# Nine transposes of the scan's decays, sums and steps into one PSUM tile, in one row, with two copies behind them

## The chip, the core and the metric

The kernel runs on one core of a Trainium2 chip, as one program in one launch. The metric is the device time in microseconds (us) of that launch; lower is better. The engines of the core work side by side, each through its own queue in order: TensorE (PE, with PEld for its weight loads), VectorE (DVE), ScalarE (ACT), GpSimd (POOL) and SyncE (SP, which here only issues transfers). They wait for each other by semaphores.

## What is computed

One layer of a streaming encoder for 256 prompt frames and 32 sample frames (288 columns together): a projection `w_in`, a pooling mixer, a state-space mixer, `w_out`, and a convolutional feed-forward part (`w_up`, `w_down`), each with RMS norms. The part around the change is the state-space scan. Cut to what matters:

```python
dt = softplus(dt_raw + dt_bias)                   # 32 heads x positions
a = dt * -exp(a_log); acum = cumsum(a)            # per chunk
lmat = exp(where(causal, acum_l - acum_s, -inf))
y_diag = einsum(cb, lmat, x * dt)                 # cb = C B^T
decay_states = exp(acum_last - acum)
states = einsum(B, decay_states, x * dt)
y = y_diag + C h_prev exp(acum) + D * x
```

## The kernel before

All activations lie with features on the 128 partitions and the 288 positions in the free dimension. A weight matrix is fetched in pieces (`raw`), split into a high part `whi` by ACT (L129) and a low part `wlo` by DVE (L130), and every 128x128 block takes three products of 288 columns (L135, L136, L137, the main stream): high with high, high with low, low with high. A piece is 128x1024 and serves 24 products. `project` runs this over column groups of 256; in the stretch of the change the groups are those of `xs` (the scan's input) and then those of `z` (its gate).

Between the products of the main stream PE does the scan's own small products in plain f32. `g` (sums of dt*A), `dt` (steps) and `dec` (decays times steps) are 32 heads by positions. The scan needs them with positions on the partitions, so nine transposes of 32 rows turn them (L412 to L414): three blocks of positions by the three quantities, the last block of `dec` from a copy of it, `dec_s` (L408). Two DVE copies per block bring them to SBUF: `tok` (sums and steps, L415) and `tokd` (decays, L416). PSUM tiles named `aux` come from a ring of three. Two other users: `pcb` (L429 to L431: the C B^T products, which DVE masks into `cbt`, L432 to L435) and `py` (L475 to L481: the scan's output).

`ssd_four(q)` does four heads. SP loads `gb` (the sums, broadcast) and `xw` (the input, positions on partitions, read back from the DRAM tile `xs_d`). DVE scales `xw` by the steps (L458). ACT forms `m` with the sums of `tok` as its bias (L463) and takes its exponential (L466), DVE multiplies it by `cbt` (L468), and PE forms `py`. The DRAM tile `xs_d` is written block by block: `conv_out` makes a tile of xs (DVE L346, L351, L352; ACT L344, L350), and `blocks_out` turns it in 32x32 blocks on DVE into the tile `blocks`, of which there is one buffer, and stores it with four transfers on SP's queue:

```python
170  s = pool_.tile([P, NT], F32, tag="blocks", bufs=1, name="blocks")
171  dve.transpose(s, src)
172  dv = d[:, t * P : (t + 1) * P].rearrange("(j r) (i f) -> i r j f", r=32, f=32)
173  for i in range(4):
174      sp.dma_start(out=dv[i], in_=s[32 * i : 32 * (i + 1), :].rearrange("r (j f) -> r j f", f=32))
```

What order the instructions take on each engine is not the order of the code. The kernel is recorded with `schedule_with_timeline_sim` set: a scheduler deals the recorded instructions into the engines' queues by a model of their times, as soon as what they read is there by that model. `tc.keep_in_program_order(ins)` binds an instruction to stay behind the one recorded before it on its engine. The queues are fixed when the program is built; on the chip nothing is reordered.

Of the kernel before, what the change touches and what calls it, by code (L numbers as in the profile page):

```python
# [16 lines left out]
P = 128  # L17
# [4 lines left out]
NT = NP_ + NS  # L22
# [3 lines left out]
HEADS = 32  # L26
# [17 lines left out]
def body(  # L44
# [25 lines left out]
    act, dve, pool, pe, sp = nc.scalar, nc.vector, nc.gpsimd, nc.tensor, nc.sync  # L70
# [11 lines left out]
    def aux(shape, name):  # L82
        return aux_ps.tile(shape, F32, tag="aux", name=name)
# [4 lines left out]
    def btile(name):  # L88
        return bpool.tile([P, NT], F32, tag="b", name=name)
# [202 lines left out]
    p_ = aux([P, NT], "pdt")  # L292
# [23 lines left out]
    id32 = ident[:HEADS, :HEADS]  # L316
# [45 lines left out]
    def htile(name, n=NT, tag=None):  # L362
        return mp.tile([HEADS, n], F32, tag=tag or name, name=name, bufs={"z": 4}.get(tag, 2) if tag else 1)
# [16 lines left out]
    dt = htile("dt", tag="gsum")  # L380
# [7 lines left out]
    g = mp.tile([HEADS, 2, MW], F32, tag="m", bufs=2, name="g")[:, 0, :]  # L388
# [11 lines left out]
    dec = htile("dec", tag="gsum")  # L400
# [4 lines left out]
    tok = mp.tile([P, 3, 2, HEADS], F32, name="tok")  # L405
    tokd = const.tile([P, 3, HEADS], F32, name="tokd")
    dec_s = mp.tile([HEADS, 4, NS], F32, name="dec_s")
    dve.tensor_copy(dec_s, dec[:, NP_:].unsqueeze(1).broadcast_to([HEADS, 4, NS]))  # L408
    dec_s = dec_s.rearrange("h r s -> h (r s)")
    for b, (go, o) in enumerate(((0, 0), (256, P), (288, NT - P))):  # L410
        p_ = aux([P, 3, HEADS], "ptok")
        pe.transpose(p_[:, 0, :], g[:, go : go + P], id32)  # L412
        pe.transpose(p_[:, 1, :], dt[:, o : o + P], id32)
        pe.transpose(p_[:, 2, :], dec_s if b == 2 else dec[:, o : o + P], id32)  # L414
        dve.tensor_copy(tok[:, b, :, :], p_[:, 0:2, :])  # L415
        dve.tensor_copy(tokd[:, b, :], p_[:, 2, :])  # L416

    bc = []
    for i in range(4):
        o = btile("bc")  # L420
# [5 lines left out]
    for gi in range(2):  # L426
        blocks_out(b_d, gi, bc[gi], mp)
        p_ = aux([P, MW], "pcb")
# [546 lines left out]
    for m in range(0, KD, 2):  # L975
        for p_ in project(wdv[:, :, 0:HALF, :], [(m * P, 256)], f[:HALF], [(0, 8), (8, 8), (16, 6)]):
            o = btile("part")
# [263 lines left out]
```

## Time and profile before

| | |
|---|---|
| median of 3 runs | 1320.14 us (1319.52 to 1320.19) |
| the profiled execution's own time | 1319.83 us |
| its span, first to last instruction | 1318.0 us |
| busy: PE / DVE / ACT / POOL | 1311.0 / 895.2 / 671.9 / 225.8 us |
| granted clock of PE over the span | 0.999 |
| the nine transposes stand between | 98.6 and 106.5 us |

A row of the trace in order of time reads: start, duration (both us, the start from the begin of the span), engine, line of the code, operation, what is written and read, shape, count; in square brackets the idle time of the engine before it and what ended that. Consecutive instructions of one line are merged in a row. PE's durations overlap: the next product starts before the last one has left the array. So the distance between two starts is what a product costs.

### The profile page before, as it was taken

How to read it: one execution, taken by the hardware profiler on the slowest of the kernel's cores; microseconds unless marked ns; L12 is line 12 of the kernel's file. 1: busy time of each engine (PE TensorE's matmuls, PEld its weight loads, DVE VectorE, ACT ScalarE, POOL GpSimd, SP SyncE). 2: the span in 40 equal slices, each digit the busy share in tenths (PEclk: the TensorE clock that was granted, in tenths of full speed). 3: DMA queues.
4: the chain of work that ended last, by engine and by line, in shares of the span. 5: the costliest groups of instructions: out<-in, count | busy, mean ns of one | idle time of the engine just before them, and what ended most of it. 6: DMA issues, size and time to landing. Idle time of an engine off the chain costs nothing.

```text
span 1318.0 us, 25197 instructions
## 1 busy us (share of the span) xinstructions
PE 1311.0 (99%) x10067; PEld 1298.9 (99%) x10067; DVE 895.2 (68%) x1486; ACT 671.9 (51%) x1010; POOL 225.8 (17%) x363
## 2 busy tenths in 40 slices
PE   9999999999999999999999999999999999999998
PEld 9999999999999999999999999999999999999997
DVE  7999988779654599977766743346666666664544
ACT  7558867446543466644444433334444454444443
POOL 6321211221430200211211200001111111101110
PEclk9999999999999999999999999999999999999999
DMA  8668874465665556666544445445444554466663
GB/s 320 209 210 283 265 235 147 151 227 205 204 216 186 181 169 220 186 184 194 174 163 161 157 171 174 155 175 181 172 160 164 179 171 160 164 235 186 204 179 109
DMA packets 104564, 249.81 MB, mean 190 GB/s; under 512 B 64224, under 2 KB 69792, under 8 KB 82176
## 3 DMA queue, kind: packets, MB, share of 16 engines
q1 hardware_dynamic: 102352, 243.44, 56.1%
q0 software_dynamic: 1664, 4.59, 1.2%
q8 instruction: 78, 1.28, 0.4%
q14 instruction: 38, 0.31, 0.1%
q10 hardware_dynamic: 432, 0.19, 0.1%
HBM read 236.23 MB, written 11.95 MB: 188 GB/s over the span
## 4 chain that ended last, share of the span: by engine, by line
PE 98%; DMA 1%; ACT 0%; DVE 0%; issue 0%; SPq 0%; ACTq 0%
PE acc L135 31%; PE acc L137 31%; PE acc L136 31%; DMA raw<-in_w_first 1%; PE py L475 1%; PE acc_x L135 1%; PE acc_x L137 1%; PE acc_x L136 1%; PE pst L772 0%; PE run_a L1113 0%; PE low L1111 0%; PE run_b L1126 0%; PE py L477 0%; PE pdt L296 0%; PE py L481 0%; PE py L479 0%
## 5 line engine op out<-in xcount | busy, mean ns | idle before, releaser
L130 DVE TENSOR_TENSOR wlo<-raw,whi 128x1024 fp32r<-128x1024 f32 (+1 forms) x386 | 463.3, 1201 | 316.0 <-ACT whi L129 313.6
L129 ACT ACTIVATE whi<-raw 128x1024 fp32r<-128x1024 f32 (+1 forms) x386 | 400.3, 1038 | 471.0 <-PE acc L136 373.9
L135 PE MATMUL acc<-hn,whi 128*128 128x288 f32 x1360 | 393.3, 294 | 0.0
L136 PE MATMUL acc<-hn,whi 128*128 128x288 f32 x1360 | 392.7, 293 | 0.0
L137 PE MATMUL acc<-hn,wlo 128*128 128x288 f32 x1360 | 392.0, 293 | 0.0
L135 PEld LDWEIGHTS acc<-hn,whi 128*128 128x128 f32 x1360 | 253.3, 188 | 0.4 <-ACT hn L872 0.4
L136 PEld LDWEIGHTS acc<-hn,whi 128*128 128x128 f32 x1360 | 253.4, 188 | 0.1
L137 PEld LDWEIGHTS acc<-hn,wlo 128*128 128x128 f32 x1360 | 253.3, 188 | 0.0
L135 PE MATMUL acc<-xn,whi 128*128 128x288 f32 x688 | 202.8, 297 | 0.6 <-ACT whi L275 0.6
L136 PE MATMUL acc<-xn,whi 128*128 128x288 f32 x688 | 200.6, 293 | 0.0
L137 PE MATMUL acc<-xn,wlo 128*128 128x288 f32 x688 | 196.0, 295 | 0.0
L135 PE MATMUL acc<-fa,whi 128*128 128x288 f32 x660 | 194.0, 294 | 0.0
L136 PE MATMUL acc<-fa,whi 128*128 128x288 f32 x660 | 193.4, 293 | 0.0
L137 PE MATMUL acc<-fa,wlo 128*128 128x288 f32 x660 | 193.1, 293 | 0.0
L135 PEld LDWEIGHTS acc<-xn,whi 128*128 128x128 f32 x688 | 129.5, 188 | 2.3 <-issue 0.9
L136 PEld LDWEIGHTS acc<-xn,whi 128*128 128x128 f32 x688 | 129.3, 188 | 0.4
L137 PEld LDWEIGHTS acc<-xn,wlo 128*128 128x128 f32 x688 | 126.9, 188 | 0.0
L135 PEld LDWEIGHTS acc<-fa,whi 128*128 128x128 f32 x660 | 124.1, 188 | 0.0
L137 PEld LDWEIGHTS acc<-fa,wlo 128*128 128x128 f32 x660 | 123.9, 188 | 0.0
L136 PEld LDWEIGHTS acc<-fa,whi 128*128 128x128 f32 x660 | 123.9, 188 | 0.0
L924 POOL COPY fc_stage<-ebuf 128x4 f32<-128x4 f32 x88 | 28.2, 320 | 521.4 <-DVE ebuf L923 521.4
L920 POOL COPY ebuf<-pf 128x2 f32<-128x2 f32 x88 | 72.3, 822 | 125.3 <-DVE fc L930 76.1
(307 smaller groups left out, 1737.6 us busy)
## 6 DMA issues: line engine op xcount, KB each, us to landing
raw<-in_w_up SPq DMA_DIRECT2D x80, 1024.0 KB, 4.8
raw<-in_w_in SPq DMA_DIRECT2D x38, 1024.0 KB, 5.0
raw<-in_w_down SPq DMA_DIRECT2D x32, 1024.0 KB, 4.7
raw<-in_w_out SPq DMA_DIRECT2D x23, 1024.0 KB, 4.8
raw<-in_w_down SPq DMA_DIRECT2D x16, 768.0 KB, 4.3
raw<-in_w_up SPq DMA_DIRECT2D x8, 896.0 KB, 4.5
gb<-g_d SPq DMA_DIRECT2D x8, 832.0 KB, 6.3
raw<-in_w_first SPq DMA_DIRECT2D x6, 768.0 KB, 8.0
```

The source lines that it names most:

```text
L129: act.activation(hi, raw[:, k : k + n, :], AF.Copy)
L130: dve.tensor_tensor(lo, raw[:, k : k + n, :], hi.bitcast(F32), op=ALU.subtract)
L135: pe.matmul(out, wh, a[:, 0, :], start=start, stop=False)
L136: pe.matmul(out, wh, a[:, 1, :], start=False, stop=False)
L137: pe.matmul(out, wl, a[:, 0, :], start=False, stop=stop)
L475: pe.matmul(y[:, 0:256], xw[:, 0, c], m[:, j, 0:256], start=True, stop=False)
L920: pool.tensor_copy(e[:, 258:260], pf[:, 4:6, i])
L924: pool.tensor_copy(fc_stage[:, :, :, i], e[:, 256:324].rearrange("p (s c) -> p s c", c=34)[:, :, 0:2])
```

## The change

The nine transposes write one PSUM tile of 128 x 3 x 3 x 32, in one fixed row: first the three of the decays, beginning with `dec_s`, then sums and steps block by block. Each but the first is bound to stay behind the one before. One copy brings all sums and steps to `tok`, one all decays to `tokd`.

```diff
-    for b, (go, o) in enumerate(((0, 0), (256, P), (288, NT - P))):
-        p_ = aux([P, 3, HEADS], "ptok")
-        pe.transpose(p_[:, 0, :], g[:, go : go + P], id32)
-        pe.transpose(p_[:, 1, :], dt[:, o : o + P], id32)
-        pe.transpose(p_[:, 2, :], dec_s if b == 2 else dec[:, o : o + P], id32)
-        dve.tensor_copy(tok[:, b, :, :], p_[:, 0:2, :])
-        dve.tensor_copy(tokd[:, b, :], p_[:, 2, :])
+    def tok_out():
+        p_ = aux([P, 3, 3, HEADS], "ptok")
+        jobs = [(2, 2, dec_s)] + [(b, 2, dec[:, P * b : P * b + P]) for b in range(2)]
+        for b, (go, o) in enumerate(((0, 0), (256, P), (288, NT - P))):
+            jobs += [(b, 0, g[:, go : go + P]), (b, 1, dt[:, o : o + P])]
+        for n, (b, i, src) in enumerate(jobs):
+            ins = pe.transpose(p_[:, b, i, :], src, id32)
+            if n:
+                tc.keep_in_program_order(ins)
+        dve.tensor_copy(tok, p_[:, :, 0:2, :])
+        dve.tensor_copy(tokd, p_[:, :, 2, :])
+
+    tok_out()
```

Six more lines of code shift the lines behind: L416 is then the transposes, L419 and L420 are the copies, and L429 becomes L435, L458 L464, L468 L474, L475 L481.

The scheduler deals the queues anew from this place on. On PE, in the group of `xs` where the transposes stand, six of the nine came before in two places:

```order
L137 MATMUL acc<-xn,wlo 128x288
L412 MATMUL ptok<-ident,g 128x32
L413 MATMUL ptok<-ident,dt 128x32
L135 MATMUL acc<-xn,whi 128x288
L412 MATMUL ptok<-ident,g 128x32
L413 MATMUL ptok<-ident,dt 128x32
L412 MATMUL ptok<-ident,g 128x32
L413 MATMUL ptok<-ident,dt 128x32
L136 MATMUL acc<-xn,whi 128x288
```

Two of the decays followed 33 products of the main stream later, and `dec_s` another 15 later. Now, six products of the main stream behind the place where `dec_s` stood:

```order
L135 MATMUL acc<-xn,whi 128x288
L416 MATMUL ptok<-ident,dec_s 128x32
L416 MATMUL ptok<-ident,dec 128x32 x2
L416 MATMUL ptok<-ident,g 128x32
L416 MATMUL ptok<-ident,dt 128x32
L416 MATMUL ptok<-ident,g 128x32
L416 MATMUL ptok<-ident,dt 128x32
L416 MATMUL ptok<-ident,g 128x32
L416 MATMUL ptok<-ident,dt 128x32
L435 MATMUL pcb<-bc 128x256
```

All nine stand together, and the six products of `pcb`, which stood 18 products of the main stream behind `dec_s`, follow at once.

On DVE, the stretch in which the product m of the first four heads stands (L468, now L474), before:

```order
L351 SCALAR_TENSOR_TENSOR xs<-tanh,conv 128x256
L352 SCALAR_TENSOR_TENSOR xs<-tanh,conv 128x32
L468 TENSOR_TENSOR m<-m,cbt 128x1664
L351 SCALAR_TENSOR_TENSOR xs<-tanh,conv 128x256
L171 STREAM_TRANSPOSE blocks<-xs 128x288
L352 SCALAR_TENSOR_TENSOR xs<-tanh,conv 128x32
L130 TENSOR_TENSOR wlo<-raw,whi 128x1024
L468 TENSOR_TENSOR m<-m,cbt 128x1664
L130 TENSOR_TENSOR wlo<-raw,whi 128x1024
L346 SCALAR_TENSOR_TENSOR conv<-ebuf_111,pah,conv 128x291
L130 TENSOR_TENSOR wlo<-raw,whi 128x1024
L171 STREAM_TRANSPOSE blocks<-xs 128x288
```

And now:

```order
L351 SCALAR_TENSOR_TENSOR xs<-tanh,conv 128x256
L352 SCALAR_TENSOR_TENSOR xs<-tanh,conv 128x32
L130 TENSOR_TENSOR wlo<-raw,whi 128x1024
L351 SCALAR_TENSOR_TENSOR xs<-tanh,conv 128x256
L352 SCALAR_TENSOR_TENSOR xs<-tanh,conv 128x32
L171 STREAM_TRANSPOSE blocks<-xs 128x288
L474 TENSOR_TENSOR m<-m,cbt 128x1664
L130 TENSOR_TENSOR wlo<-raw,whi 128x1024
L171 STREAM_TRANSPOSE blocks<-xs 128x288
```

The first m moved behind the turning of the second tile of its pair, and the turning after that follows closer; the second m comes further on. Further up in the same queue the two copies stand six rows later than the first pair of the old ones did: behind four steps of the convolution, the product for `ce` and one more weight piece.

The third place is `py` of heads 4 to 7 on PE. Before it stood in two halves with main stream between them, each of them:

```order
L135 MATMUL acc<-xn,whi 128x288
L475 MATMUL py<-m,xw 64x256 x2
L477 MATMUL py<-m,xw 64x128 x2
L479 MATMUL py<-m,xw 64x32 x2
L481 MATMUL py<-ce,h0t 64x32 x2
L136 MATMUL acc<-xn,whi 128x288
```

Now it is one piece:

```order
L135 MATMUL acc<-xn,whi 128x288
L481 MATMUL py<-m,xw 64x256 x4
L483 MATMUL py<-m,xw 64x128 x4
L485 MATMUL py<-m,xw 64x32 x4
L487 MATMUL py<-ce,h0t 64x32 x4
L136 MATMUL acc<-xn,whi 128x288
```

The `py` of the first four heads stands eleven products of the main stream further on than before. From the `py` of heads 8 to 11 on, PE's small products stand within one product of their old places in the main stream.

## The prediction

> **What bounds the kernel now.** I read the page first, then the busy time by window, then the order of time of PE and of DVE around the change, and last the waits of DVE.
>
> ```profile
> span 1318.0 us, 25197 instructions
> PE 1311.0 (99%) x10067; PEld 1298.9 (99%) x10067; DVE 895.2 (68%) x1486; ACT 671.9 (51%) x1010; POOL 225.8 (17%) x363
> PE 98%; DMA 1%; ACT 0%; DVE 0%; issue 0%; SPq 0%; ACTq 0%
> ...
> 125.00:155.00 30.00, 30.00 (x268) 28.76 (x265) 26.99 (x50) 26.65 (x58) 6.22 (x7) 1.00 0.85 269
> ...
> 183.00:213.00 30.00, 30.00 (x247) 29.51 (x247) 29.36 (x44) 20.32 (x40) 9.12 (x8) 1.00 0.63 192
> ```
>
> The first three lines say that PE sets the time: 99% busy, 98% of the chain that ended last. So a cut of PE's own work counts in full, and any wait that reaches PE counts in full too. The two rows by window (PE, weight load, DVE, ACT, POOL busy, then clock and DMA share) say where such a wait could come from. DVE is 68% busy as a mean, but from 183 to 213 us it works 29.36 of 30.00 us. There it has nothing left with which to make up for being late.
>
> **What the change takes off PE.** A product of the main stream with 288 columns starts every 0.131 us: in the rows below 24 steps lie between 100.72 and 103.86. What an insertion costs is the distance between a product before it and a product two places behind it, less the steps of the main stream in between.
>
> ```profile
> 98.40 0.29 PE L137 MATMUL acc<-xn,wlo 128*128 128x288 f32 x1
> ...
> 99.92 0.30 PE L135 MATMUL acc<-xn,whi 128*128 128x288 f32 x1
> ...
> 100.72 0.29 PE L135 MATMUL acc<-xn,whi 128*128 128x288 f32 x1
> ...
> 103.86 0.29 PE L135 MATMUL acc<-xn,whi 128*128 128x288 f32 x1
> 104.09 0.31 PE L414 MATMUL ptok<-ident,dec 32*128 32x32 f32 x2
> ...
> 104.69 0.30 PE L135 MATMUL acc<-xn,whi 128*128 128x288 f32 x1
> ...
> 106.28 0.29 PE L135 MATMUL acc<-xn,whi 128*128 128x288 f32 x1
> 106.51 0.24 PE L414 MATMUL ptok<-ident,dec_s 32*128 32x32 f32 x1
> ...
> 107.05 0.29 PE L135 MATMUL acc<-xn,whi 128*128 128x288 f32 x1
> ```
>
> One transpose alone costs 107.05 - 106.28 - 3 x 0.131 = 0.38 us, two together 104.69 - 103.86 - 0.39 = 0.44. So a transpose is 0.06 and the leaving and re-entering of the main stream 0.32. The six in two insertions (98.40 to 99.92, four steps) test this: 1.52 - 0.52 = 1.00, and 2 x 0.32 + 6 x 0.06 = 1.00. Before, the nine stand in four insertions: 1.82 us. In a row they cost 0.32 + 9 x 0.06 = 0.86: **0.96 us less**. In the new order the row stands directly ahead of the six pcb products. Whether it shares the price of the insertion with them is read from another neighbour pair:
>
> ```profile
> 213.50 0.29 PE L137 MATMUL acc<-xn,wlo 128*128 128x288 f32 x1
> ...
> 216.34 0.29 PE L136 MATMUL acc<-xn,whi 128*128 128x288 f32 x1
> ...
> 270.65 0.29 PE L137 MATMUL acc<-xn,wlo 128*128 128x288 f32 x1
> ...
> 271.40 0.29 PE L136 MATMUL acc<-xn,whi 128*128 128x288 f32 x1
> ```
>
> psum_g alone (128*128, like the main stream) costs 271.40 - 270.65 - 0.26 = 0.49. Directly behind a py insertion (128*64) the pair costs 216.34 - 213.50 - 0.26 = 2.58, which is the 2.09 of py alone (below) and again 0.49. Standing next to each other saved nothing, so I count nothing for the neighbourhood of pcb. [...] Had the price hung on leaving the stream at all, the nine would save 4 x 0.32 = 1.28 instead of 0.96.
>
> The order also puts together one py group of four heads that now stands in two halves.
>
> ```profile
> 123.12 0.29 PE L136 MATMUL acc<-xn,whi 128*128 128x288 f32 x1
> 123.34 1.08 PE L475 MATMUL py<-m,xw 128*64 128x256 f32 x8
> ...
> 125.47 0.30 PE L135 MATMUL acc<-xn,whi 128*128 128x288 f32 x1
> ...
> 125.87 0.29 PE L135 MATMUL acc<-xn,whi 128*128 128x288 f32 x1
> ...
> 127.33 0.29 PE L137 MATMUL acc<-xn,wlo 128*128 128x288 f32 x1
> ...
> 131.02 0.29 PE L135 MATMUL acc<-xn,whi 128*128 128x288 f32 x1
> ...
> 132.49 0.30 PE L137 MATMUL acc<-xn,wlo 128*128 128x288 f32 x1
> ```
>
> A whole group costs 125.47 - 123.12 - 0.26 = 2.09, the halves 1.20 and 1.21: **0.32 us less**. PE's own work shrinks by 0.96 + 0.32 = 1.28 us.
>
> **What it does to DVE.** Six copies become two. Each has three times the columns of an old one.
>
> ```profile
> L415 DVE COPY tok<-ptok 128x64 f32<-128x64 f32 x3 | 0.6, 202 | 0.0
> L416 DVE COPY tokd<-ptok 128x32 f32<-128x32 f32 x3 | 0.5, 168 | 0.0
> ```
>
> The trace has no copy of 192 or 96 columns of this tile. The pair takes at least as long as an old pair (0.37) and at most as long as three (1.11); so 0 to 0.74 us of DVE are saved, about 0.4 by the middle. DVE is not the chain that ends last, so this counts only where DVE is late. What counts more is the place. The copies now wait for all nine transposes and stand behind another weight piece, ce and four convolution steps. ACT's relu of the first heads, the product m (L468) and py follow from them.
>
> ```profile
> 98.62 0.48 DVE L171 STREAM_TRANSPOSE blocks<-xs 128x288 f32<-128x288 f32 x1 [2.19 <-DMA xs_d<-blocks]
> ...
> 103.79 0.21 DVE L408 COPY dec_s<-dec 32x128 f32<-32x128 f32 x1
> 103.93 0.41 DVE L351 SCALAR_TENSOR_TENSOR xs<-tanh,conv 128x256 f32<-128x256 f32 x1
> ...
> 104.76 1.17 DVE L130 TENSOR_TENSOR wlo<-raw,whi 128x1024 fp32r<-128x1024 f32 x1
> ...
> 114.97 0.48 DVE L171 STREAM_TRANSPOSE blocks<-xs 128x288 f32<-128x288 f32 x1
> ...
> 117.92 1.89 DVE L468 TENSOR_TENSOR m<-m,cbt 128x1664 f32<-128x1664 f32 x1
> ...
> 120.65 0.48 DVE L171 STREAM_TRANSPOSE blocks<-xs 128x288 f32<-128x288 f32 x1 [0.52 <-DMA xs_d<-blocks]
> ```
>
> There is one blocks buffer, so a transposition into it (L171) waits until the four stores of the one before have landed. Here that took 120.65 - 114.97 = 5.68 us, and DVE stood for the last 0.52. Before, m runs ahead of this second L171, at 117.92. In the new order m stands behind it. With the first L171 where it was, m starts at 114.97 + 5.68 + 0.41 = 121.06, **3.1 us later**. Ahead of it DVE has then done one more pair L351, L352 and one more L171 (104.76 - 103.93 = 0.83 us from start to start), less the 0.4 of the copies; so against equal work it is 3.1 - 0.4 = 2.7 us behind. py itself still has room: it had 123.34 - 119.81 = 3.5 us behind m, and now, with eleven products more ahead of it (+1.44) and 0.96 saved, 123.82 - 122.95 = 0.9.
>
> Does DVE catch up? Its waits from 100 to 213 us:
>
> ```profile
> DVE xw L458 <- DMA xw<-xs_d: 5.5, 3, 3.0
> DVE blocks L171 <- DMA xs_d<-blocks: 2.4, 2, 1.8
> ```
>
> These 7.9 us are all the room there is. But xw is read back from what blocks stored, and a store is issued after its L171: if DVE is late, so are these transfers, and the waits move along with it. The new order also makes a second wait. Behind the late m comes one weight piece and then already the next L171: from L171 to L171 that is 0.41 + 1.81 + 1.15 = 3.4 us of DVE's work (from start to start), where before a piece, m, a piece, a convolution step and a piece lay between, 5.8. If the stores take their 5.68 us again, DVE stands 2.3 us there; if they land within the work, it stands not at all. Bounds for the lateness on entering the full stretch at 183: 0 (all absorbed) and 2.7 + 2.3 and twice more the 2.19 of 98.62, 9.4. I take the two waits that the order shows, 2.7 + 2.3 = **5.0**: it is the sum of what can be counted off, and nothing between them and 183 is free of the stores.
>
> **What PE can bear.** The weight pieces (wlo, L130) that DVE ends just before PE needs them:
>
> ```profile
> 197.97 1.83 DVE L130 TENSOR_TENSOR wlo<-raw,whi 128x1024 fp32r<-128x1024 f32 x1
> ...
> 201.31 0.29 PE L137 MATMUL acc<-xn,wlo 128*128 128x288 f32 x1
> ...
> 202.14 1.22 DVE L130 TENSOR_TENSOR wlo<-raw,whi 128x1024 fp32r<-128x1024 f32 x1
> ...
> 204.46 0.29 PE L137 MATMUL acc<-xn,wlo 128*128 128x288 f32 x1
> ```
>
> The two L137 are the first that read these pieces (a piece serves 24 products, 3.15 us). The first ended at 199.80 and was read at 201.31, the second at 203.36 and 204.46: margins of 1.51 and 1.10 us. PE now arrives 1.28 us sooner, but where it must wait for DVE this is lost: the second piece ends 5.0 us later, so PE passes it 5.0 - 1.1 = 3.9 us later than before. No other term is added, since the shorter PE work lies ahead of this point. Against the profiled execution's 1319.83 this gives 1323.7 (the median of the runs shown is 0.31 above that execution). What a measurement of this kernel can tell from no change is about 0.2%, 2.6 us.
>
> **Rivals.** (a) Not slower: DVE's lateness is taken up by its 7.9 us of waits before 183, and PE keeps its 1.28: 1318.55. It decides from a lateness under 1.1 us at the piece of 203.36. For it: every wait of DVE in the stretch is for a transfer. Against it: those transfers start behind DVE's own transpositions. 0.15. (b) The waits for the stores repeat: lateness 9.4, less 1.1, so 8.3 more: 1328.1. For it speaks a DMA share of 0.85 from 125 to 155. 0.12. (c) PE stands at the row of transposes, because its first one reads dec_s. That is ready at 104.00; PE, six products further on than before, arrives at 106.28 - 1.00 - 0.44 + 0.79 = 105.63. The margin is 1.6; two weight pieces in between (2.4) would make PE wait 0.8: 1319.35. The order leaves dec_s where it was. 0.02. (d) Faster by over 0.2%: 2.6 us where 1.28 were found. PE has no wait in this stretch that could end, so another 1.5 us would have to come from elsewhere: 1317.0. 0.05.
>
> **How the numbers follow.** The forecast has 0.66. With its lateness anywhere from 2.5 to 7 it spans 1321.2 to 1325.7; 0.07 of its 0.66 lie within 0.2%. Slower: 0.59 + 0.12 = 0.71. Within 0.2%: 0.07 + 0.15 + 0.02 = 0.24. Faster: 0.05. The range goes from rival (a) to (b): 1318.3, the 0.3 of one insertion under (a), to 1328.1.
>
> **What would show it.** Right: PE idle before L137 on a DVE weight piece near 200 us, some 5 us in all; the first m at about 121 and a wait of L171 soon after it; nine transposes in about 0.9 us. If PE has no wait between 110 and 215, the step of the lateness is wrong and (a) holds. A wait at py near 123.8 would mean that the stores take longer than 5.68. A wait at the first transpose is (c).

## The result, and the profile after

| | before | after |
|---|---|---|
| median | 1320.21 us (21 runs, 1319.23 to 1321.32) | 1323.29 us (21 runs, 1320.78 to 1326.66) |
| ratio, with its 95% interval | | 1.0023 (1.0017 to 1.0029) |
| profiled execution: own time, span | 1319.83, 1318.0 us | 1324.24, 1321.7 us |

The changed kernel is slower by 3.1 us at the median, 0.23%, and its executions scatter over 5.9 us where the old ones scatter over 2.1. Its page and its busy time by window (PE, weight load, DVE, ACT and POOL busy, then granted clock, DMA share, GB/s):

```profile
PE 1312.2 (99%) x10067; PEld 1300.1 (98%) x10067; DVE 894.5 (68%) x1482; ACT 670.3 (51%) x1010; POOL 220.9 (17%) x363
...
183.00:213.00 30.00, 27.13 (x209) 26.18 (x209) 27.59 (x44) 19.23 (x40) 9.29 (x8) 0.94 0.59 179
```

From 95 to 183 us PE has no wait. From 183 to 213 it is busy for 27.13 of 30.00 us where it was busy throughout, and the granted clock there is 0.94 instead of 1.00. So two things are lost in one place. First the gain, on PE in order of time (start, duration, engine, line, operation, names, shape, count):

```profile
105.64 0.29 PE L135 MATMUL acc<-xn,whi 128*128 128x288 f32 x1
105.86 0.24 PE L416 MATMUL ptok<-ident,dec_s 32*128 32x32 f32 x1
...
106.54 0.70 PE L435 MATMUL pcb<-bc 128*128 128x256 f32 x2
...
108.53 0.29 PE L137 MATMUL acc<-xn,wlo 128*128 128x288 f32 x1
```

The row follows its product at once. From the product ahead of it to the second one behind pcb pass 108.53 - 105.64 = 2.89 us; less two steps of 0.131, row and pcb together cost 2.63. Then the place of the loss:

```profile
199.75 0.29 PE L137 MATMUL acc<-xn,wlo 128*128 128x288 f32 x1
200.49 0.40 PE L135 MATMUL acc<-xn,whi 128*128 128x288 f32 x1 [0.45 <-ACT whi L129]
200.73 0.29 PE L136 MATMUL acc<-xn,whi 128*128 128x288 f32 x1
203.44 0.40 PE L137 MATMUL acc<-xn,wlo 128*128 128x288 f32 x1 [2.42 <-DVE wlo L130]
203.68 0.29 PE L135 MATMUL acc<-xn,whi 128*128 128x288 f32 x1
...
204.13 0.45 PE L135 MATMUL acc<-xn,whi 128*128 128x288 f32 x1
204.37 0.45 PE L136 MATMUL acc<-xn,whi 128*128 128x288 f32 x1
...
207.25 0.37 PE L136 MATMUL acc<-xn,whi 128*128 128x288 f32 x1
207.46 0.29 PE L137 MATMUL acc<-xn,wlo 128*128 128x288 f32 x1
```

One fetch of 1 MB is split in two halves of 128x1024; these are the weight pieces of the prediction. PE stands for the first half of the first fetch of the fifth z group: for its high part (whi, from ACT) and then, much longer, for its low part (wlo, from DVE). From 199.75 to 200.49 and from 200.73 to 203.44 pass 0.74 + 2.71 us where a step is 0.131 each: **3.2 us lost by waiting**. Then, from 204.13 to 207.25, products start every 0.24 us: 13 of them lose 13 x 0.11 = 1.4 us, with the two half-slow steps beside them **1.6**. The windows there show why (columns as above; the granted clock is the third number from the end):

```profile
200.58:203.99 3.41, 0.99 (x6) 0.76 (x7) 3.38 (x5) 3.41 (x6) 2.28 (x2) 1.00 0.15 37
203.99:207.40 3.41, 3.41 (x16) 3.41 (x16) 3.41 (x2) 1.77 (x2) 2.39 (x2) 0.50 0.01 2
```

The granted clock falls to a half at 203.99, some 0.6 us after PE has begun to work again at 203.44, and is back at 207.40. The first product behind each of the two waits also takes 0.24 us, 0.2 more for both. Ahead of all this PE has gained 1.2 us: the product at 199.75 stood at 200.92 before. So 3.2 + 1.6 + 0.2 - 1.2 = 3.8 us are found, for the 3.7 between the spans.

DVE and its waits in the stretch (for each row of waits: us in total, times, longest), and ACT's first row that reads the new copies:

```profile
109.20 0.34 DVE L419 COPY tok<-ptok 128x192 f32<-128x192 f32 x1
109.46 0.23 DVE L420 COPY tokd<-ptok 128x96 f32<-128x96 f32 x1
...
120.34 0.48 DVE L171 STREAM_TRANSPOSE blocks<-xs 128x288 f32<-128x288 f32 x1 [2.12 <-DMA xs_d<-blocks]
120.74 1.85 DVE L474 TENSOR_TENSOR m<-m,cbt 128x1664 f32<-128x1664 f32 x1
...
124.03 0.48 DVE L171 STREAM_TRANSPOSE blocks<-xs 128x288 f32<-128x288 f32 x1 [0.30 <-DMA xs_d<-blocks]
...
174.48 0.48 DVE L171 STREAM_TRANSPOSE blocks<-xs 128x288 f32<-128x288 f32 x1 [0.19 <-DMA xs_d<-blocks]
...
184.71 0.48 DVE L171 STREAM_TRANSPOSE blocks<-xs 128x288 f32<-128x288 f32 x1 [2.92 <-DMA xs_d<-blocks]
...
202.17 1.22 DVE L130 TENSOR_TENSOR wlo<-raw,whi 128x1024 fp32r<-128x1024 f32 x1
```

```profile
109.57 4.64 ACT L469 ACTIVATE m<-gb,tok 128x256 f32<-128x256 f32 x15 [0.83 <-DVE tok L419]
117.94 1.58 ACT L472 ACTIVATE m<-m 128x1664 f32<-128x1664 f32 x1
```

```profile
DVE blocks L171 <- DMA xs_d<-blocks: 9.6, 8, 2.9
DVE xw L464 <- DMA xw<-xs_d: 4.6, 3, 1.8
```

The first of these rows in the kernel before, from 95 to 213 us as above:

```profile
DVE blocks L171 <- DMA xs_d<-blocks: 4.6, 3, 2.2
```

m starts at 120.74 instead of 117.92. The piece at 202.17 ends at 203.39; before, it ended at 199.80. The waits for stores have grown from 4.6 us in three to 9.6 in eight. The longest, 2.92 us, is for the stores of xs tile 12, which was turned at 174.48: the next L171 could start only 10.2 us after. SP's queue shows what stands ahead of them (L114 fetches 1 MB of weights):

```profile
175.49 0.38 SPq L114 DMA_DIRECT2D raw<-in_w_in  x1
175.96 3.38 SPq L174 DMA_DIRECT2D xs_d<-blocks  x4
```

The same pair stands in the kernel before, and there too L171 starts only 10.0 us after the one before it. SP's queue and DVE of that kernel:

```profile
173.18 0.38 SPq L114 DMA_DIRECT2D raw<-in_w_in  x1
173.66 3.31 SPq L174 DMA_DIRECT2D xs_d<-blocks  x4
...
172.31 0.47 DVE L171 STREAM_TRANSPOSE blocks<-xs 128x288 f32<-128x288 f32 x1
182.31 0.48 DVE L171 STREAM_TRANSPOSE blocks<-xs 128x288 f32<-128x288 f32 x1 [1.84 <-DMA xs_d<-blocks]
```

So the long landing is not new. DVE already comes 2.2 us later to the L171 of tile 12 (174.48), and is still 2.4 later at the next one (184.71): between the two it cannot catch up, since the stores set the pace.

### The profile page after: what moved, and what is told of

The parts are those of the page before. It is cut to its first block, busy times and chain, and to the rows that moved or that the text cites. A ratio compares the mean times of both kernels' runs of the same rounds, so it can differ in the third digit from the quotient of the medians.

```text
span 1321.7 us, 25194 instructions
## 1 busy us (share of the span) xinstructions
PE 1312.2 (99%) x10067; PEld 1300.1 (98%) x10067; DVE 894.5 (68%) x1482; ACT 670.3 (51%) x1010; POOL 220.9 (17%) x363
## 3 DMA queue, kind: packets, MB, share of 16 engines
q8 instruction: 78, 1.28, 0.4%
## 4 chain that ended last, share of the span: by engine, by line
PE 97%; DMA 1%; DVE 1%; ACT 0%; issue 0%; SPq 0%; ACTq 0%
PE acc L137 31%; PE acc L135 31%; PE acc L136 30%; DMA raw<-in_w_first 1%; PE py L481 1%; PE acc_x L135 1%; PE acc_x L137 1%; PE acc_x L136 1%; PE pst L778 0%; PE run_a L1119 0%; PE low L1117 0%; PE run_b L1132 0%; PE py L483 0%; DVE wlo L130 0%; PE pdt L296 0%
## 5 line engine op out<-in xcount | busy, mean ns | idle before, releaser
L130 DVE TENSOR_TENSOR wlo<-raw,whi 128x1024 fp32r<-128x1024 f32 (+1 forms) x386 | 463.0, 1201 | 314.9 <-ACT whi L129 312.6
L129 ACT ACTIVATE whi<-raw 128x1024 fp32r<-128x1024 f32 (+1 forms) x386 | 399.9, 1037 | 466.4 <-PE acc L136 367.3
L936 DVE SCALAR_TENSOR_TENSOR fc<-ebuf,pf,fc 128x290 f32<-128x290 f32 x176 | 90.0, 517 | 2.7
```

The lines of the kernel that those rows point to most:

```text
L129: act.activation(hi, raw[:, k : k + n, :], AF.Copy)
L130: dve.tensor_tensor(lo, raw[:, k : k + n, :], hi.bitcast(F32), op=ALU.subtract)
L936: dve.scalar_tensor_tensor(c, e[:, r_ : r_ + 290], pf[:, r_, i : i + 1], c, op0=ALU.mult, op1=ALU.add)
```

## The experiments

Eight kernels are the changed one or the old one with edits of order, two take over a part of the change, one fills a wait and one makes waits of many lengths. Times are medians; in brackets is the ratio to the kernel before, run beside it, with its 95% interval, and then the fastest and slowest execution. The changed kernel itself was not run again beside them; the old kernel's medians in these batches lie from 1319.86 to 1320.17. Each kernel was profiled in one execution, which need not be a typical one; its time is given where it lies far from the median. Added lines shift the numbers of lines: L171, L130 and L474 of the changed kernel stand a few lines further down in some of them. An edit of order can also make the scheduler deal other instructions anew behind it.

### The first m ahead of the L171 again

```diff
-            blocks_out(xs_d, 2 * i + j, o, mp)
+            with ExitStack() as order:
+                if (i, j) == (3, 0):
+                    order.enter_context(tc.issue_after(ms[0].ins))
+                blocks_out(xs_d, 2 * i + j, o, mp)
```

`ms[0]` is the first L474; `issue_after` puts what the block records behind it on its engine.

> The changed kernel with one more edge: the transposition into blocks of xs tile 6 (L171) is issued behind the first m instead of ahead of it, as it was before the change. Theory (DVE gets late because m stands behind that L171 and its wait for the stores, and the lateness reaches the weight piece near 200 us): m starts about 3 us earlier, near 118; PE's wait for wlo near 200 shrinks from 2.4 us to under 0.5, the granted clock in 183 to 213 us is 1.00 again, and the time is the change's saving alone, about 1318.9 (ratio to before 0.999). Rival (the lateness is made later, by the waits of L171 from 165 to 190 us, and the first m has no part in it): PE's wait stays at 2 to 3 us and the time at about 1323.

1322.65 us (1.0015, 1.0006 to 1.0024), 1318.76 to 1326.06. Neither half of what the theory expected came, and the time is the rival's. m did not start near 118, and PE still stood for 1.59 us. DVE and PE of this kernel:

```profile
120.23 1.89 DVE L475 TENSOR_TENSOR m<-m,cbt 128x1664 f32<-128x1664 f32 x1 [1.85 <-ACT m L473]
```

```profile
204.83 0.40 PE L137 MATMUL acc<-xn,wlo 128*128 128x288 f32 x1 [1.59 <-DVE wlo L130]
205.07 0.30 PE L135 MATMUL acc<-xn,whi 128*128 128x288 f32 x1
205.20 0.30 PE L136 MATMUL acc<-xn,whi 128*128 128x288 f32 x1
```

With the L171 out of the way, m waits for ACT's exponential. In the changed kernel that ends at 117.94 + 1.58 = 119.52, so the L171 held m up by at most 1.2 of the 2.8 us. The rest comes from `tok`: the wide copy is made at 109.20, where the first two of the narrow ones stood at 105.86 and 106.09 and ACT's relu could begin at 107.32 instead of 109.57. Behind this wait of 1.59 us the first product takes 0.24 us (204.83 to 205.07) and the next ones 0.131. The wait is at the second half of the fetch, not at the first as in the changed kernel. From this L171 on DVE's order differs from the changed kernel's in other places too, and the profiled execution took 1320.37 us, 2.3 less than the median. So the run shows that the place of m is not the whole cause, and not where its median is lost.

### The old kernel with m behind the L171

The same edge the other way round, in the old kernel: the conversion of xs tile 6 is recorded early and the first m issued behind its L171.

```diff
+        if i == 3:
+            xs_conv(3, (0,))
...
+            if q == 0:
+                order.enter_context(tc.issue_after(turned[-1].ins))
             dve.tensor_tensor(m, m, cbt[:, gi : gi + 1, :].broadcast_to([P, 4, MW]), op=ALU.mult)
```

> The kernel before, with its old transposes and copies, and one edge more: the first m is issued behind the transposition of xs tile 6 into blocks (L171), as in the changed kernel. Theory of the prediction (m behind that L171 makes DVE 3 us late, and this is carried to 200 us): PE waits for wlo near 200, 1 to 3 us, and the time is 1321 to 1324. Rival (the place of the first m matters little, since later waits for stores set DVE's pace): no wait of PE over 0.5 us, 1319.5 to 1320.5.

1320.58 us (1.0004, 0.9996 to 1.0013), 1319.37 to 1323.78; m started at 121.60, later than in the changed kernel, and in the profiled execution (1320.01 us) PE waited for no weight piece, only 0.4 us at py. The rival's case: a first m that is over 3 us late does not reach 200 us by itself. But PE had gained nothing here, so its margins of 1.51 and 1.10 us were whole; and the slowest execution, 1323.78, was not profiled.

### Six copies behind the row, and the row with the old tiles

```diff
-        dve.tensor_copy(tok, p_[:, :, 0:2, :])
-        dve.tensor_copy(tokd, p_[:, :, 2, :])
+        for b in range(3):
+            dve.tensor_copy(tok[:, b, :, :], p_[:, b, 0:2, :])
+            dve.tensor_copy(tokd[:, b, :], p_[:, b, 2, :])
```

> The changed kernel with its row of nine transposes and its one PSUM tile, but six narrow copies behind them, as before, in place of the two wide ones. Theory (the loss comes from the order that the row gives DVE): in this order too the L171 of xs tile 6 stands ahead of the first m, so PE's wait near 200 us stays, 1 to 3.5 us, and the time is 1321 to 1324. Rival (the wide copies are what makes DVE late, since each waits for all nine transposes): the wait is gone, about 1319.3, which is before less the 1.3 saved on PE and with the old 0.4 us of copies.

1322.74 us (1.0019, 1.0007 to 1.0031), 1318.18 to 1327.98. The wide copies are not what makes it slow: it is as slow with six narrow ones. Here the first tok copy stands at 109.65; it is the row that makes them late, not their width. The profiled execution took 1319.84 us, 2.9 less than the median; in it PE waits 0.25 and 0.74 us at the two halves.

In the second kernel only the row is taken over, with three tiles and six copies as before:

```diff
-        p_ = aux([P, 3, 3, HEADS], "ptok")
+        ps = [aux([P, 3, HEADS], "ptok") for _ in range(3)]
...
-            ins = pe.transpose(p_[:, b, i, :], src, id32)
+            ins = pe.transpose(ps[b][:, i, :], src, id32)
```

> The kernel before with one part of the change alone: its three PSUM tiles and six copies stay, but the nine transposes are bound in a row in the changed kernel's sequence. Theory: PE gains the same 0.95 us at the transposes, DVE has the L171 of xs tile 6 ahead of the first m as in the changed kernel, and PE waits 0.9 to 3 us for wlo near 200: 1320.5 to 1323.5. Rival (the one wide tile is the cause): 1319.0.

1320.32 us (1.0000, 0.9992 to 1.0009), 1318.44 to 1322.69, a little under what was expected; in the profiled execution, which took 1321.93 us, PE waits 0.76 and 0.72 us at the two halves. So the row alone wins nothing in the median: it gives back what it saves. But it does not lose the 3 us either, though its tok copies come at 109.25, as late as the changed kernel's 109.20. So late copies alone do not make the kernel slow. What the single PSUM tile adds is not settled: DVE's order differs between the two kernels in many places from 109 us on.

### A filled wait

```diff
+        for n in range(fill[0]):
+            pe.matmul(accs[0], acts[0][:, 0, 0:P], acts[0][:, 0, :], start=True, stop=True)
```

`fill[0]` is 18 for the fifth z group and 0 elsewhere.

> The changed kernel with 18 products more on PE (xn by xn, into the accumulator that is then started anew; their result is discarded), just ahead of the products of the z group whose weight piece is late near 200 us: 18 x 0.131 = 2.36 us of work where PE otherwise stands for 2.6. Theory (the products behind the wait run at 0.24 us because PE had stood still; the granted clock follows PE's idle time): PE has no wait of over 0.7 us, the products behind it run at 0.131, the granted clock in 183 to 213 us is 1.00, and the time falls by 1.8 to about 1321.5, though 2.4 us of work were added. Rival (the clock or the products are slow there for another reason): the slow products stay, and the time is 1323.3 or more; if the 18 products do not fall into the wait, 1325.7.

1323.25 us (1.0024, 1.0014 to 1.0034), 1321.95 to 1325.03. The time did not fall by 1.8. In its profile PE waits 0.85 and 0.75 us, the granted clock is 1.00 and no product is slow, as the theory has it; but DVE was later there than in the changed kernel's profile (12.0 us of waits for stores against 9.6). 2.4 us of work were added at no change of the median, and the scatter was 3.1 us in nine executions against 5.9 in 21. That is in keeping with the clock, and no proof of it.

### The clock by itself

```diff
+    more_of = {100: 5, 110: 6, 120: 7, 130: 8, 140: 9, 150: 10, 160: 12, 170: 14}
...
+                for _ in range(1 + more_of.get(nth[0], 0)):
-                act.activation(hi, raw[:, k : k + n, :], AF.Copy)
+                    act.activation(hi, raw[:, k : k + n, :], AF.Copy)
```

> The kernel before with ACT's copy of eight weight pieces far apart, behind 300 us, repeated 6 to 15 times, so that PE stands for whi in eight steps of different length; it computes the same. It measures one thing: how PE's products run behind a wait of a given length. Theory (after a wait of over about 2 us the granted clock is lowered, and products take 0.24 instead of 0.131 us for about 4 us): behind the short waits (under 2 us) the products take 0.131 at once, behind each longer one about 16 of them take 0.24, so each costs its length and about 1.8 us more. Rival (the slow products near 204 us had another cause): they run at 0.131 behind waits of any length.

One execution: 1382.74 us, with seven waits for whi from 0.46 to 11.2 us. Two of them on PE, and the windows of the second:

```profile
412.35 0.40 PE L139 MATMUL acc<-mixs,whi 128*128 128x288 f32 x1 [0.46 <-ACT whi L132]
...
413.61 0.40 PE L141 MATMUL acc<-mixs,wlo 128*128 128x288 f32 x1 [0.47 <-DVE wlo L134]
413.85 0.30 PE L139 MATMUL acc<-mixs,whi 128*128 128x288 f32 x1
413.98 0.29 PE L140 MATMUL acc<-mixs,whi 128*128 128x288 f32 x1
```

```profile
446.83 0.40 PE L139 MATMUL acc<-mixp,whi 128*128 128x288 f32 x1 [1.43 <-ACT whi L132]
...
448.10 0.58 PE L141 MATMUL acc<-mixp,wlo 128*128 128x288 f32 x1 [0.46 <-DVE wlo L134]
448.47 0.45 PE L139 MATMUL acc<-mixp,whi 128*128 128x288 f32 x1
...
451.35 0.40 PE L141 MATMUL acc<-mixp,wlo 128*128 128x288 f32 x1
```

```profile
444.75:448.16 3.41, 1.52 (x10) 1.04 (x9) 1.34 (x2) 2.00 (x2) 0.00 (x0) 1.00 0.00 0
448.16:451.57 3.41, 3.41 (x14) 3.41 (x15) 3.29 (x3) 0.00 (x0) 0.00 (x0) 0.50 0.36 89
```

Behind 0.46 and 0.47 us nothing is slow but the first product, 0.24 us; the next ones take 0.13, at a clock of 1.00. Behind 1.43 and 0.46, 1.27 us apart, products start every 0.24 us from 448.47 to 451.35, at a clock of 0.50. Around two of the longer waits the clock is 0.50 throughout: from 538 to 541 us (PE busy for 1.33 of 3.00) and from 620 to 624 (0.25 of 4.00), and in 541 to 545 and 624 to 628 behind them PE has 16 products in 4.00 us, one per 0.25. So in this run a lower clock follows PE's standing still, as the theory has it, but the theory's 2 us, the author's estimate, do not hold: behind 1.43 with 0.46 the clock was 0.50, behind the 1.59 above 1.00, and 1.00 also behind a wait of 2.01 in a kernel below. What decides is not shown; the last section sets these waits side by side.

### The fetch behind the stores

The decisive one: the load of weights ahead of tile 12's four stores goes behind them. On PE, DVE and ACT nothing is moved.

```diff
+            if kb in behind:
+                order.enter_context(tc.issue_after(behind.pop(kb).ins))
             sp.dma_start(out=raw, in_=view[:, c0 // 256, kb : kb + nk, :nc_])
```

`behind` holds the last store of tile 12 for the first load of the fifth z group, and nothing else.

> The changed kernel with one exchange in SP's queue and nothing else: the 1 MB weight load that stood right ahead of the four stores of xs tile 12 (issued at 175.49 us, the stores from 175.96 on) goes right behind them. In the changed kernel these stores take until 184.71 to land, 10.2 us after their L171, and DVE stands for 2.92 us. Theory (DVE's lateness at the weight piece near 200 us is set by how long these stores take to land, behind that load): the next L171 starts at 181 to 182.5 instead of 184.71, DVE's wait there is under 1 us, PE's wait for wlo near 200 is under 0.7, and the time falls by 2 us or more, to 1318.8 to 1321, with less scatter. Rival (the lateness is already there from the order at 115 to 125 us, and the store is only where it shows): PE's wait stays over 1.5 us and the time at about 1323. Rival (the load itself comes too late then): PE waits for whi or raw of that piece, 1323 or more.

1320.23 us (1.0004, 0.9996 to 1.0013), 1318.87 to 1322.65: **3.1 us less than the changed kernel** by the medians, 2.5 by the two ratios to the old kernel, whose intervals do not meet; and that by one exchange of two neighbours in a queue. SP's queue and DVE of this kernel (L174 is L180 here, L114 L118, L171 L177):

```profile
175.84 1.88 SPq L180 DMA_DIRECT2D xs_d<-blocks  x4
177.76 3.34 SPq L118 DMA_DIRECT2D raw<-in_w_in  x2
```

```profile
174.84 0.48 DVE L177 STREAM_TRANSPOSE blocks<-xs 128x288 f32<-128x288 f32 x1 [0.74 <-DMA xs_d<-blocks]
181.51 0.47 DVE L177 STREAM_TRANSPOSE blocks<-xs 128x288 f32<-128x288 f32 x1
```

The four stores are issued in 1.88 us instead of 3.38, and the next L171 comes 6.7 us after the one before it, without a wait, instead of 10.2. PE's wait falls to 0.72 us, at the second half of the fetch, and the clock stays at 1.00. PE and DVE have the same order as in the changed kernel. DVE is no earlier at tile 12 (174.84 against 174.48, and 172.31 in the old kernel); it catches up at the next L171, 181.51 against 182.31 in the old kernel. So the exchange does not remove what makes DVE late ahead of tile 12; it lets DVE make up for it in time.

The control is the same exchange in the old kernel:

> The same exchange in SP's queue, in the kernel before, as a control. Theory: DVE's wait at 182.31 shrinks (1.84 us before), but PE waited for nothing near 200 us and its work is as before, so the time is the same, 1319.5 to 1320.2. Rival (the exchange speeds something else up, or costs something): it moves by 1 us or more here too.

1320.08 us (1.0000, 0.9991 to 1.0009). DVE has no wait at that L171 any more (177.80 instead of 182.31), and the time does not move: PE waited for no weight piece there.

### What else stands ahead of the piece

`xw`, `ce` and m of the seventh group of four heads, and ACT's work for them, are issued behind both halves of the weight fetch; the load ahead of tile 12's stores stays where the changed kernel has it.

```diff
+            if q == 6:
+                for ins in halves[z4[0] + 1]:
+                    order.enter_context(tc.issue_after(ins.ins))
```

`halves[z4[0] + 1]` are L129 and L130 of the second half.

> The changed kernel with the second edit alone: the seventh group's work behind the two tight pieces, and the weight load still ahead of tile 12's stores. Theory: DVE stays as late behind the stores (2 to 3 us of wait for them near 184 us), but xw, ce and m no longer stand ahead of the two pieces (0.94 + 0.89 us ahead of the first, 2.5 more ahead of the second), so PE's wait is under 1.5 us, the clock is not lowered, and the time is 1319.5 to 1321.5. Rival (ACT is as late as DVE, and whi ends last): 1322 or more, with PE waiting for whi.

1320.83 us (1.0007, 0.9999 to 1.0016), 1319.74 to 1324.72. DVE stood for 3.59 us at that L171 in the profiled execution, and PE still for 2.01. The row of PE and the two windows around it:

```profile
202.14 0.40 PE L141 MATMUL acc<-xn,wlo 128*128 128x288 f32 x1 [2.01 <-DVE wlo L133]
...
197.88:201.30 3.42, 2.25 (x18) 2.03 (x16) 3.42 (x8) 2.00 (x4) 1.77 (x3) 1.00 0.97 305
201.30:204.71 3.41, 2.57 (x19) 2.57 (x20) 3.04 (x3) 3.41 (x11) 3.13 (x2) 1.00 0.06 11
```

More than the 1.5 expected, with no slow clock behind it: the window after these two has 1.00 as well; the time is within its bounds. With the load moved as well:

> The changed kernel with the weight load behind the stores of tile 12, as in the run before, and also with ACT's and DVE's work for the seventh group of four heads (exponentials, ce, xw, m: 1.8 us and 2.5 us on DVE) issued behind the two halves of the weight piece that PE waits for near 200 us. Theory (the row saves PE 1.27 us, and all that was lost is DVE's lateness at those two pieces, with the clock behind it): no wait of PE from 110 to 300 us, granted clock 1.00, and the median is that of before less 1.3, 1318.6 to 1319.1, ratio 0.999, with no more scatter than before (2 us). Rival (something else in the change costs as well): no wait of PE there, but 1320 or more. Rival (the work put back makes PE wait later, at py near 214 us or at a later piece): 1320 or more with that wait in the profile.

1319.28 us (0.9995, 0.9986 to 1.0004), 1318.69 to 1323.07. The profiled execution has no wait of PE from 95 to 300 us and a span of 1317.3. Five of twelve executions lie from 1318.69 to 1318.99, under the fastest of the 28 of the old kernel beside them (1319.50); two lie over 1320.5.

> The kernel before with both of these changes of order, but its own transposes and copies: the control. Theory: PE waited for nothing there, so the same time as before, 1319.5 to 1320.3; the difference to the changed kernel with the same two edits is then the row's own worth, 1.3 us. Rival (the edits are worth something by themselves): 1319.0 or less.

1320.13 us (0.9996, 0.9987 to 1.0005). Without the row the two edits are worth nothing that can be measured.

### All three edits of order

> The changed kernel with both mends of the run before (the weight load behind tile 12's stores; the seventh group's work behind the two tight pieces) and also the L171 of xs tile 6 behind the first m. Theory (the rest of the scatter comes from DVE's lateness in those executions in which stores land late, and each place that is mended takes some of it): no wait of PE near 200 us, median 1318.7 to 1319.2, ratio to before 0.999 or under, and few executions over 1320. Rival (the third edit adds nothing, since the first m's place was worth little in the other runs): as with the two mends, 1319.3 and the same scatter; or a new wait elsewhere, over 1319.6.

**1319.14 us (0.9991, 0.9982 to 1.0000)**, 1318.45 to 1319.81: a scatter of 1.4 us in eleven executions. The median is 1.0 us under the old kernel's beside it, but the interval of the ratio just reaches 1. From the two edits above it differs by 0.14 us, which tells nothing about the third edit; three of twelve executions were over 1320 there and none is here. Its page, a window, and a landmark on PE (the product ahead of a py, which the kernel before has at 213.50):

```profile
span 1316.7 us, 25194 instructions
...
183.00:213.00 30.00, 30.00 (x248) 29.21 (x248) 27.00 (x42) 19.62 (x42) 7.80 (x8) 1.00 0.62 183
...
212.28 0.29 PE L144 MATMUL acc<-xn,wlo 128*128 128x288 f32 x1
```

PE is 213.50 - 212.28 = 1.22 us ahead at this point, and the span is 1318.0 - 1316.7 = 1.3 shorter: what the row and the joined py save.

## Why the prediction was right, and where it was not

Forecast 1323.7 us, measured 1323.29: slower, by a late piece of DVE near 200 us. Its terms one by one:

- **PE's gain, 1.28 us: right.** The row's 0.86 by its sum and the 1.75 of pcb alone in the old trace (109.04 to 111.05, less two steps) make 2.61; row and pcb together took 2.63. Standing next to pcb saved nothing, as the neighbour pair said. Why it costs the same next to pcb is not shown. The kernel without waits shows the gain, 1.2.
- **The copies: right in size, their place not priced.** 0.34 + 0.23 us, between its bounds of 0.37 and 1.11. But the sum has them as DVE's work alone. That ACT's relu follows from them it said and did not price: tok comes 3.1 us later (106.09 to 109.20), ACT's relu 2.3 later, the first exponential 1.8 (116.14 to 117.94).
- **m 3.1 us later, at 121.06: the number held (120.74, 2.8 later), its cause only in part.** With the L171 moved away m started at 120.23, and the old kernel with m behind the L171 loses nothing that can be measured. The prediction's 7.9 us of DVE's waits leave out one of 0.4 for ACT (wlo, L130); this changes nothing in its sum.
- **A second wait of 2.3 us soon after it: wrong.** It was 0.30 at 124.03; the stores landed within 3.7 us. "If the stores take their 5.68 us again" was the step that failed: landing times differ. Behind a 1 MB fetch it was 10.2, ahead of it at most 6.7, and that wait, 2.92 us at 184.71, was not foreseen, though the old trace has one of 1.84 at the same place. Why the stores at 120.34 landed as early as 3.7 is not shown.
- **Lateness 5.0 at the piece: too large, and the path in part another.** The first half was 203.39 - 199.80 = 3.6 us late, and PE waited there (margin 1.51), not at the second half (1.10) as forecast. What makes DVE 2.2 us late ahead of tile 12 is not taken apart further by any run.
- **PE idle of some 5 us in all: 3.2.** Most of what was missing was made up by the lowered clock, 1.6 us, of which the prediction had nothing. So two errors of nearly the same size, some 2 us too much of waiting and 1.6 of clock left out, stand behind the good agreement of the sum; that they cancel is luck. PE passed the second half 208.25 - 204.46 = 3.8 us later than before, where 3.9 was forecast, but by this other path.

Rival (a), the lateness absorbed, is nearly what the kernel with all three edits does (1318.55 forecast, 1319.14 measured). In the changed kernel it failed at the stores of tile 12, with 10.2 us the longest landing that a wait shows in the stretch, right ahead of the part in which DVE has almost no idle time. Rival (b): the waits for stores did repeat, eight times, but the lateness was 3.6 and not 9.4; what the slowest executions (up to 1326.66) waited for no profile shows. Rival (c) did not occur: the first transpose followed its product at once.

That the scatter has the same cause is argued, not shown: in the changed kernel the margins are used up by PE's 1.2 us and DVE's 2 to 4, so each difference in landing would reach the time. The old kernel's executions lie within 2.1 us in the first batch and within 1.7 to 4.0 in the later ones, so the 1.4 of eleven executions with all three edits is not clearly less. That landing times differ from one execution to the next is seen in few profiles only: up to tile 12's stores the changed kernel, the one with the filled wait and the one with the late group have the same order on DVE, and they waited there for 2.92, 3.17 and 3.59 us.

## What to carry to other kernels

- Where PE is the bound and another engine feeds it just in time, work saved on PE is worth at most the margin of the next piece, unless that engine is made earlier as well: read that margin (end of the piece, start of its first reader) before counting the saving. Here 1.28 us met margins of 1.51 and 1.10.
- A transposed tile with a single buffer makes its engine wait for the landing of its stores (2.92 us at 184.71 here), so their place in the transfer queue counts: put small stores that someone waits for ahead of a large prefetch that nobody needs yet. One such exchange was worth some 3 us here, and nothing in the kernel whose margin was whole.

## What was not expected of the hardware

The granted clock fell to a half behind these short waits and not in them: it was 0.50 from 203.99 to 207.40 in the changed kernel and from 448.16 to 451.57 in the kernel of the waits, 3.41 us each time, and 1.00 in the 3.41 us ahead of both. In those PE stood for 2.42 us (200.58:203.99) and for 1.89 (444.75:448.16; 1.43 and 0.46 together), 3.41 less its busy time in the rows above.

With the late group PE stood for 1.17 us in 197.88:201.30 and for 0.84 in 201.30:204.71, in its one wait of 2.01, and the clock stayed at 1.00; behind the one of 1.59 with m ahead it stayed at 1.00 too. What decides between these cases is not shown. So here products ran at 0.13 us behind a wait of 2.01, and one of 2.42 with 0.45 ahead of it cost 1.6 us more in slow products.

Four stores of one tile, 36 KB each, had landed 3.7 us after their L171 at 120.34 and 10.2 us after the one at 174.48, in one and the same kernel.
